# The norm's Rsqrt, its spread and the first two scaled chunks given first rank in the order of issue

## The chip, the cores and the metric

The kernel runs on one core of a Trainium2 chip. A core has engines with a queue each: TensorE (PE; its weight loads are shown apart as PEld), VectorE (DVE), ScalarE (ACT), GpSimd (POOL) and SyncE (SP), which issues most of the DMAs. The metric is device time in microseconds for one execution; less is better.

## The reference

Two layers over 256 latent tokens and 256 context tokens, 1024 wide, all in float32. `h` is the latent stream and `hc` the context stream; both go through the same weights with their own shifts and scales, and in the second layer the context stream ends after it has given its keys and values.

```python
def rms_norm(x, g):
    y = xf * lax.rsqrt(jnp.mean(xf * xf, axis=-1, keepdims=True) + EPS)
    return (y * g.astype(jnp.float32)).astype(x.dtype)
...
for l in range(DEPTH):
    h = h + 0.5 * gt1 * swiglu(modulate(rms_norm(h, g_ffn1[l]), sh1, sc1), *ffn1)
    px = modulate(rms_norm(h, g_mix[l]), sh2, sc2) @ w_in[l]
    ...   # two attentions and a long convolution on px
    h = h + gt2 * (jnp.concatenate([ya, yb, yc], axis=-1) @ w_out[l])
    h = h + 0.5 * gt3 * swiglu(modulate(rms_norm(h, g_ffn2[l]), sh3, sc3), *ffn2)
    ...   # the same for hc
```

Each feed-forward block and each mixer thus begins with an RMS norm of its input, a scale and a shift. The change touches the five norms behind the first one.

## The kernel before

**Layout.** The activations lie transposed: `self.h` holds 8 chunks (`j`) of 128 features by 512 tokens; columns 0 to 255 are stream 0 (latent), 256 to 511 stream 1 (context). Every big product is made of three matmuls in a rounded format (`mm3`, L352 to L354): high part of the weights by high part of the activations (`whi`, `xh`), high by low (`xl`), low (`wlo`) by high. `prefetch` (L323) loads weight tiles of 2048 columns (`raw`, two buffers, DMA on SP) and splits them in halves of 1024 columns: ScalarE casts `whi` (L337), VectorE subtracts for `wlo` (L338); there are four buffers of each, so that a half can be split up to four ahead of its use (`next_half`).

**The norm.** `residual` (L447, VectorE) adds a block's product to `h`; `add_square` squares the new chunk on ScalarE (L370) and adds the squares on POOL (L374). `measure` sums over the partitions with small matmuls (L385) and makes 1/rms with 11 VectorE instructions on 128 x 2 numbers (L387, L68 to L78). `spread` (L390) writes each 128 tokens' 1/rms on a diagonal (`dg`, L397, two instructions) and multiplies it with ones on TensorE (L398), so that each partition has the row `rb`. `modulate` (L428) makes, for each chunk `j`, `xn` (L439, VectorE: h by scale by `rb`), `xh` (L441, ScalarE: plus shift, rounded) and `xl` (L442, VectorE: what the rounding left).

**Order around a norm.** In the last part of a feed-forward block (`ffn`, tiles m = 2 and 3 of the down product) and of the first mixer (`mix`) stream 0 is computed ahead of stream 1, so that stream 0's norm can run beside stream 1's products: `measure(0)` and `spread(0)` stand between stream 1's products, chunks 0 to 3 of `modulate` right behind `spread(0)`, chunks 4 to 7 behind the block. Stream 1's norm hangs on hooks in the next block's first products (`pair_of_blocks`). The last mixer has stream 0 alone and does its norm in one piece at the end (`alone`). The five norms are: end of the first feed-forward block, of the first mixer, of the second and third feed-forward block, of the second mixer.

**Who orders the instructions.** The program text is a list; a planner turns it into one queue for each engine at build time. It goes through the program with its own model of times: whenever an engine is free in that model, it gets, among the instructions whose inputs and buffers are ready, the one with the lowest rank. The rank is the place in the text. Once built, an engine works its queue strictly in that order. Products go to PSUM tiles `mm` (four buffers), the norm's sums and `rb` to tiles `aux` (four buffers).

Of the kernel before, what the change touches and what calls it, by code (L numbers as in the profile page):

```python
# [41 lines left out]
class Net:  # L42
# [361 lines left out]
    def norm(self, l, which, alone=False):  # L404


        r, rb = {}, {}

        def measure(s):
            r[s] = self.measure((s,), [self.acc_tile], self.apart)  # L410

        def spread(s):
            rb[s], _ = self.spread(r[s], 2)

        def modulate(s, js):
            self.modulate(l, which, s, rb[s], js)

        if alone:
            measure(0)
            spread(0)  # L420
            modulate(0, range(ND))
            return
        self.hooks = {"measure": lambda: measure(1), "spread": lambda: spread(1), "modulate": lambda: modulate(1, range(ND))}
        return {"measure": lambda: measure(0), "spread": lambda: (spread(0), modulate(0, range(4))),
                "end": lambda: modulate(0, range(4, ND))}
# [679 lines left out]
```

## Time and profile before

| | |
|---|---|
| median of 3 runs | 1767.94 us (1767.07 to 1768.29) |
| profiled execution | 1770.06 us |
| its span, first to last instruction | 1767.4 us |
| mean granted clock of TensorE | 0.995 |
| PE busy | 1727.5 us, 98% |
| DVE busy | 1143.6 us, 65% |
| ACT busy | 649.2 us, 37% |
| POOL busy | 91.6 us, 5% |
| DMA | 251.95 MB, 143 GB/s in the mean |

The busy time counts what an engine executes; what it spends waiting for others stands beside the instruction that ended the wait. The five norms lie around 411, 663, 1031, 1407 and 1567 us of the span. A granted clock of 1.00 is 2.4 GHz, 0.50 is 1.2 GHz.

### The profile page before, as it was taken

To read this page: it belongs to the slowest core of one execution; us is meant where nothing else is said; L and a number is where in the kernel's file an instruction comes from. 1 tells how busy PE (TensorE), PEld (TensorE's weight loads), DVE (VectorE), ACT (ScalarE), POOL (GpSimd) and SP (SyncE) were. 2 spreads that over 40 slices of the span, in tenths; PEclk is the share of its full clock that TensorE was granted. 3 is DMA by queue.
4 is the path that set the end of the run, shared out by engine and by line. 5 is a ranking of instruction groups with operands and counts; after the bars stand their busy time and mean duration, and the time that the engine had idled before them with its cause. 6 is when DMAs were issued, how large, how long until landed. Compare 5 with 4: busy or idle time off the path is not lost.

```text
span 1767.4 us, 24959 instructions
## 1 busy us (share of the span) xinstructions
PE 1727.5 (98%) x9996; PEld 1479.5 (84%) x9996; DVE 1143.6 (65%) x2218; ACT 649.2 (37%) x1053; POOL 91.6 (5%) x128
## 2 busy tenths in 40 slices
PE   7999999999999999999999999999999999989999
PEld 3787888889897689888888898888888998789999
DVE  4778778757657868666676475554543587865554
ACT  4422222234337744212222342222222445744443
POOL 0000000011200020000000110000000311010000
PEclk9999999999999999999999999999999999989999
DMA  7765555532221023544544335434432233135554
GB/s 265 295 194 179 178 181 204 182 125 72 84 72 37 25 103 123 175 163 167 163 167 143 108 122 188 170 131 144 153 131 90 91 130 108 49 119 171 182 185 131
DMA packets 47430, 251.95 MB, mean 143 GB/s; under 512 B 6000, under 2 KB 7234, under 8 KB 29522
## 3 DMA queue, kind: packets, MB, share of 16 engines
q1 hardware_dynamic: 47106, 250.26, 41.0%
q8 instruction: 78, 1.28, 0.3%
q14 instruction: 38, 0.30, 0.1%
q0 software_dynamic: 64, 0.10, 0.0%
q10 hardware_dynamic: 144, 0.01, 0.0%
HBM read 249.30 MB, written 1.05 MB: 142 GB/s over the span
## 4 chain that ended last, share of the span: by engine, by line
PE 89%; DVE 7%; ACT 2%; issue 1%; DMA 1%; POOL 0%; POOLq 0%; ACTq 0%; DVEq 0%
PE mm L352 26%; PE mm L353 26%; PE mm L354 25%; DVE wlo L338 2%; PE mm L680 2%; PE mm L682 2%; PE mm L681 2%; PE aux L903 1%; PE aux L896 1%; ACT whi L337 1%; PE aux L613 1%; PE mm L872 1%; DMA raw<-wgu 0%; PE aux L125 0%; PE mm L878 0%
## 5 line engine op out<-in xcount | busy, mean ns | idle before, releaser
L352 PE MATMUL mm<-xh,whi 128*128 128x512 f32 (+1 forms) x1760 | 608.4, 350 | 9.0 <-ACT xh L441 3.8
L353 PE MATMUL mm<-xl,whi 128*128 128x512 f32 (+1 forms) x1760 | 611.0, 348 | 3.0 <-DVE xl L442 2.0
L354 PE MATMUL mm<-xh,wlo 128*128 128x512 f32 (+1 forms) x1760 | 609.9, 348 | 0.0
L338 DVE TENSOR_TENSOR wlo<-raw,whi 128x1024 fp32r<-128x1024 f32 x324 | 387.3, 1197 | 226.4 <-ACT whi L337 223.6
L337 ACT CAST whi<-raw 128x1024 fp32r<-128x1024 f32 x324 | 332.3, 1027 | 535.3 <-PE mm L353 356.8
L352 PEld LDWEIGHTS mm<-xh,whi 128*128 128x128 f32 x1760 | 332.7, 191 | 55.3 <-ACT xh L201 6.4
L353 PEld LDWEIGHTS mm<-xl,whi 128*128 128x128 f32 x1760 | 335.5, 191 | 46.8 <-DVE xl L442 2.6
L354 PEld LDWEIGHTS mm<-xh,wlo 128*128 128x128 f32 x1760 | 335.0, 191 | 42.1 <-issue 2.2
L352 PE MATMUL mm<-hh,whi 128*128 128x512 f32 (+1 forms) x788 | 271.3, 344 | 0.0
L353 PE MATMUL mm<-hl,whi 128*128 128x512 f32 (+1 forms) x788 | 271.2, 344 | 0.1
L354 PE MATMUL mm<-hh,wlo 128*128 128x512 f32 (+1 forms) x788 | 270.5, 343 | 0.0
L505 DVE TENSOR_TENSOR gs<-gs,mm 128x512 f32<-128x512 f32 (+1 forms) x88 | 54.6, 621 | 186.4 <-ACT gs L504 148.0
L352 PEld LDWEIGHTS mm<-hh,whi 128*128 128x128 f32 x788 | 149.3, 190 | 19.2 <-issue 1.9
L353 PEld LDWEIGHTS mm<-hl,whi 128*128 128x128 f32 x788 | 149.4, 190 | 18.9 <-issue 1.1
L354 PEld LDWEIGHTS mm<-hh,wlo 128*128 128x128 f32 x788 | 149.3, 189 | 17.3
L447 DVE SCALAR_TENSOR_TENSOR h<-mm,mod,h 128x256 f32<-128x256 f32 x216 | 98.7, 479 | 92.1 <-PE mm L354 91.4
L285 DVE CUSTOM_DVE_ANT_0 ada<-ada,cb 128x1024 f32<-128x1024 f32 x128 | 156.0, 1221 | 2.1
L504 ACT ACTIVATE gs<-mm 128x512 f32<-128x512 f32 (+1 forms) x88 | 47.8, 544 | 275.1 <-PE mm L354 271.2
L285 DVE CUSTOM_DVE_ANT_0 prod<-ada,cb 128x1024 f32<-128x1024 f32 x96 | 117.0, 1219 | 0.0
L374 POOL TENSOR_TENSOR acc<-acc,sq 128x256 f32<-128x256 f32 x61 | 52.5, 867 | 1237.0 <-ACT sq L370 1198.2
L680 PE MATMUL mm<-whi,xh 128*128 128x256 f32 x336 | 98.0, 292 | 0.0
L681 PE MATMUL mm<-wlo,xh 128*128 128x256 f32 x336 | 96.1, 286 | 0.0
(178 smaller groups left out, 1442.9 us busy)
## 6 DMA issues: line engine op xcount, KB each, us to landing
raw<-wgu SPq DMA_DIRECT2D x86, 1024.0 KB, 4.9
ada<-wada SPq DMA_DIRECT2D x128, 512.0 KB, 3.6
raw<-wd SPq DMA_DIRECT2D x32, 896.0 KB, 4.6
raw<-wd SPq DMA_DIRECT2D x16, 1024.0 KB, 4.9
raw<-win SPq DMA_DIRECT2D x12, 1024.0 KB, 4.8
a<-wada SPq DMA_DIRECT2D x8, 1024.0 KB, 5.0
raw<-wout SPq DMA_DIRECT2D x8, 1024.0 KB, 4.8
raw<-why SPq DMA_DIRECT2D x6, 1024.0 KB, 4.8
```

The lines of the kernel that those rows point to most:

```text
L285: nc.vector.tensor_tensor_reduce(out=prod, in0=w, in1=self.cb[:, s], scale=1.0, scalar=0.0, op0=ALU.mult, op1=ALU.add, accum_out=m[:, s, j ...
L337: nc.scalar.copy(hi[:, :n], raw)
L338: nc.vector.tensor_tensor(out=lo[:, :n], in0=raw, in1=hi[:, :n].bitcast(F32), op=ALU.subtract)
L352: t.matmul(out, whi, xhi, start=start, stop=False)
L353: t.matmul(out, whi, xlo, start=False, stop=False)
L354: t.matmul(out, wlo, xhi, start=False, stop=stop)
L374: nc.gpsimd.tensor_tensor(out=self.acc[s], in0=self.acc[s], in1=sq, op=ALU.add)
L447: return self.nc.vector.scalar_tensor_tensor(out=self.h[:, j, cols], in0=ps[:, c0:c0 + SEQ], scalar=self.mod(l, ch, s, j), in1=self.h[:, j ...
L504: nc.scalar.activation(gs[:, :n], pg[:, :n], AF.Silu)
L505: nc.vector.tensor_tensor(out=gs[:, :n], in0=gs[:, :n], in1=pu[:, :n], op=ALU.mult)
L680: nc.tensor.matmul(out, self.xh[:, kk, t], hi[:, w], start=kk == 0 and i == 0, stop=False)
L681: nc.tensor.matmul(out, self.xh[:, kk, t], lo[:, w], start=False, stop=False)
```

## The change

`high_priority()` gives all that is created inside it the rank of the start of the program, in place of its rank in the text. The change puts `measure` and `spread` of every norm in it, of both streams, and chunks 0 and 1 of stream 0's `modulate`. The first norm of all (`first_norm`) calls the inner `measure` and `spread` itself and isn't touched; nor are the squares, their sums, the residual sums, casts and splits. The instructions, their data and their buffers are the same.

```diff
         def measure(s):
-            r[s] = self.measure((s,), [self.acc_tile], self.apart)
+            with self.tc.high_priority():
+                r[s] = self.measure((s,), [self.acc_tile], self.apart)
 
         def spread(s):
-            rb[s], _ = self.spread(r[s], 2)
+            with self.tc.high_priority():
+                rb[s], _ = self.spread(r[s], 2)
 
         def modulate(s, js):
+            if s == 0 and js[0] == 0:
+                with self.tc.high_priority():
+                    self.modulate(l, which, s, rb[s], js[:2])
+                js = js[2:]
             self.modulate(l, which, s, rb[s], js)
```

## Rows read from the trace of the kernel before

**Rows 1.** The profile page, busy time of each engine in the whole span.
```profile
PE 1727.5 (98%) x9996; PEld 1479.5 (84%) x9996; DVE 1143.6 (65%) x2218; ACT 649.2 (37%) x1053; POOL 91.6 (5%) x128
```

**Rows 2.** Waits of PE: who waited for whom, total us, times, longest.
```profile
PE aux L398 <- DVE dg L397: 4.3, 3, 2.6
PE mm L352 <- ACT xh L441: 3.8, 5, 1.6
...
PE mm L353 <- DVE xl L442: 2.0, 3, 0.7
...
PE aux L385 <- POOL acc L374: 1.4, 1, 1.4
```

**Rows 3.** Windows: us; busy (count) of PE, PEld, DVE, ACT, POOL; PEclk; DMA.
```profile
395.00:425.00 30.00, 28.81 (x237) 28.20 (x236) 20.73 (x58) 11.36 (x21) 9.00 (x15) 1.00 0.22 77
650.00:680.00 30.00, 26.98 (x208) 26.25 (x207) 23.51 (x62) 12.84 (x25) 8.80 (x8) 0.94 0.20 70
...
664.00:667.00 3.00, 3.00 (x17) 3.00 (x15) 1.50 (x5) 1.16 (x3) 0.73 (x1) 0.50 0.00 0
```

**Rows 4.** Timeline of DVE, first seam: start, us, what, [idle before <- releaser].
```profile
405.09 0.28 DVE L397 TENSOR_SCALAR dg<-ident,rsy 128x128 f32<-128x128 f32 x1
405.29 2.35 DVE L338 TENSOR_TENSOR wlo<-raw,whi 128x1024 fp32r<-128x1024 f32 x2
407.56 0.87 DVE L447 SCALAR_TENSOR_TENSOR h<-mm,mod,h 128x256 f32<-128x256 f32 x2
408.35 0.28 DVE L397 TENSOR_SCALAR dg<-ident,rsy 128x128 f32<-128x128 f32 x1
409.21 0.87 DVE L439 SCALAR_TENSOR_TENSOR xn<-h,mod,aux 128x256 f32<-128x256 f32 x2 [0.58 <-PE aux L398]
410.76 1.23 DVE L338 TENSOR_TENSOR wlo<-raw,whi 128x1024 fp32r<-128x1024 f32 x1 [0.68 <-ACT whi L337]
411.91 1.00 DVE L442 SCALAR_TENSOR_TENSOR xl<-xn,mod,xh 128x256 fp32r<-128x256 f32 x2
```

**Rows 5.** Timeline of PE, first seam.
```profile
411.19 0.62 PE L352 MATMUL mm<-xh,whi 128*128 128x256 f32 x3 [0.36 <-ACT xh L441]
412.51 0.39 PE L353 MATMUL mm<-xl,whi 128*128 128x256 f32 x1 [0.70 <-DVE xl L442]
```

**Rows 6.** Timeline of PE, second seam (end of the first mixer).
```profile
658.02 0.39 PE L352 MATMUL mm<-xh,whi 128*128 128x256 f32 x1 [0.62 <-DVE h L447]
...
660.90 0.49 PE L398 MATMUL aux<-dg,ones 128*128 128x128 f32 x2 [0.82 <-DVE dg L397]
661.14 0.36 PE L352 MATMUL mm<-xh,whi 128*128 128x256 f32 x1
...
663.55 0.88 PE L352 MATMUL mm<-xh,whi 128*128 128x256 f32 x4 [1.57 <-ACT xh L441]
```

**Rows 7.** Timeline of DVE, second seam.
```profile
652.96 0.15 DVE L387 TENSOR_SCALAR ms<-aux 128x2 f32<-128x2 f32 x1
...
657.41 0.16 DVE L75 SCALAR_TENSOR_TENSOR rsy<-rsu,rsy 128x2 f32<-128x2 f32 x1
657.49 0.48 DVE L447 SCALAR_TENSOR_TENSOR h<-mm,mod,h 128x256 f32<-128x256 f32 x1
...
659.01 0.70 DVE L76 TENSOR_TENSOR rst<-rsy 128x2 f32<-128x2 f32 x1
...
661.35 1.22 DVE L338 TENSOR_TENSOR wlo<-raw,whi 128x1024 fp32r<-128x1024 f32 x1
662.48 0.86 DVE L439 SCALAR_TENSOR_TENSOR xn<-h,mod,aux 128x256 f32<-128x256 f32 x2
```

**Rows 8.** Timeline of DVE, last norm: the first and the last of 13 instructions.
```profile
1564.46 0.16 DVE L387 TENSOR_SCALAR ms<-aux 128x2 f32<-128x2 f32 x1 [0.52 <-PE aux L385]
...
1566.63 0.48 DVE L397 TENSOR_SCALAR dg<-ident,rsy 128x128 f32<-128x128 f32 x2
```

**Rows 9.** Timeline of POOL, second seam.
```profile
657.96 2.55 POOL L374 TENSOR_TENSOR acc<-acc,sq 128x256 f32<-128x256 f32 x2 [1.66 <-ACT sq L370]
```

## The prediction

> **What bounds the kernel now.** I read the page first: TensorE is busy for 98% of the span [rows 1], so the change can only win what TensorE loses around the norms. The list of waits, kept to TensorE, says what that is. Three of its lines belong to the norms: the diagonal `dg` behind `spread` (4.3 us), the scaled chunk `xh` (3.8 us) and its low part `xl` (2.0 us); no line of that list names a weight split [rows 2]. I then put stretches of 30 us around the seams (a seam: the end of one block, the norm, the start of the next) side by side: TensorE idles 30 − 28.81 = 1.19 us around the first, 3.02 us around the second, where its granted clock is 0.94 in the mean [rows 3].
>
> The order on VectorE explains the idle time at the first seam. The first half of `dg` starts at 405.09; then come two weight splits (2.35 us) and two residual sums (0.87 us), and only then the second half, at 408.35 [rows 4]. The two scaled chunks `xn` start at 409.21. Then a third split, released by ScalarE's cast, runs 1.23 us ahead of `xl` [rows 4]. TensorE loses 0.36 us until `xh` is there and 0.70 us until `xl` is [rows 5]. There are three waits for `xl`, 2.0 us in all [rows 2]: the three norms that end a feed-forward block go alike, and lose 3 × 0.36 + 2.0 = 3.1 us.
>
> The second seam (end of the first mixer) loses three pieces: 0.62 us for a residual sum, 0.82 us for `dg`, 1.57 us for `xh`, together 3.01 us [rows 6]. Here the Rsqrt chain itself is cut up: from its first instruction at 652.96 to the end of `xn` at 663.34 pass 10.4 us [rows 7]. The same chain in the last norm, with nothing between, takes from 1564.46 to 1567.11, 2.65 us [rows 8]. Behind these idle pieces the granted clock is 0.50, 1.2 GHz in place of 2.4; a mean of 0.94 over 30 us is 0.06 × 30 = 1.8 us of matmul time lost [rows 3]. This seam therefore costs 3.0 + 1.8 = 4.8 us.
>
> In the norm of the last mixer TensorE waits 2.6 us for `dg`, the longest of that line, and 1.4 us for a sum of squares on POOL [rows 2], but there the chain already runs without anything between.
>
> **The change part by part.** No instruction is added or removed, and none of the moved ones issues a DMA. What moves are, for each norm of each stream (nine in all), the measuring matmuls, 11 small VectorE instructions, two `dg` and the spreading matmuls, and for stream 0 two `xn`, `xh` and `xl`. They pass the weight splits and residual sums on VectorE, casts and squares on ScalarE, and the big matmuls in TensorE's queue; POOL's and SP's queues keep their instructions, but a weight load that waits for a delayed split goes out later by as much. I price that at nothing: the splits feed halves that lie up to four ahead, and TensorE waits for none now. Without that cover one delayed split costs its 1.2 us [rows 4].
>
> *Feed-forward seams (three).* From `dg` at 405.09 the new order on VectorE should be: both `dg` (0.48, as in [rows 8]), one split while TensorE spreads (1.2), two `xn` (0.87), the other split while ScalarE casts `xh` (1.2), two `xl` (0.9): 405.09 + 4.65 = 409.7, against 412.91 now. TensorE comes free at 411.19 − 0.36 = 410.83 [rows 5], so `xh` and `xl` of the first two chunks are there and 0.36 + 0.70 us can go. What is late next: the two residual sums (0.87) slide to 410.6 and free the accumulators late, and the third split still waits for its cast and ends near 412. TensorE bridges that with what it has, but chunks 2 and 3 follow on VectorE a split later. I leave 0.3 us per seam: 3.1 − 0.9 = 2.2 us. Bounds: nothing, if the residual sums take the whole wait over, and 3.1.
>
> *First mixer's seam.* Moving ahead does not keep the chain together: an instruction that waits for the one just before it leaves its engine free, and a ready one steps in, as the residual sum at 657.49 does behind the chain's instruction at 657.41 [rows 7]. I expect the first two splits to go on cutting in. What falls behind the chain is the third split (1.22 us, between `dg` and `xn`) and the residual sum beside it (0.48): 1.7 us earlier for `xn`, about the 1.57 us that TensorE waits for `xh`. The 0.62 and 0.82 us I leave: the first hangs on a residual sum, the second on the chain's middle. With idle time falling from 3.0 to about 1.4 us the clock may stay up: at the first seam 1.19 us of idle time leaves it at 1.00 [rows 3]. I take half of the 1.8 us. Together 1.57 + 0.9 = 2.5 us; bounds nothing and 4.8.
>
> One of the chain's instructions takes 0.70 us where its neighbour, as small, takes 0.16; a POOL sum of squares runs from 657.96 at the same time [rows 7, 9]. In the sum that stays as it is, since the POOL sums don't move. The Trainium skill (SBUF — State Buffer, section Who interferes with whom) has a VectorE instruction with two SBUF inputs wait for a whole POOL instruction that reads SBUF. By that rule a chain that runs earlier only meets other POOL sums, and the seam would give 1.57 us and no clock: 0.9 us less in all, 1764.6.
>
> *Earlier matmuls in TensorE's queue.* A measuring or spreading matmul now enters as soon as the planner thinks its input ready; where it thinks too early, everything behind it waits. At the second seam it already does so: the spreading matmul holds TensorE for 0.82 us, and the big matmuls behind it then run with no wait of their own [rows 6]. Lower bound nothing, upper bound 0.82 for each of about 12 such places, 9.8. I take 0.5 us in all, nearer to nothing, because the same order at the first seam leaves no such wait of note in the list [rows 2].
>
> *Second streams and the last norm.* TensorE waits for no second stream's norm now, so their earlier chains win nothing; they cost VectorE 2.65 us each earlier, hidden as long as chunks 2 to 7 keep ahead. The last norm's chain is clean [rows 8], and it begins when POOL's sum of squares and the squares are there, which don't move: nothing. Its 2.6 us are the chain itself.
>
> **Sum.** 2.2 + 2.5 − 0.5 = 4.2 us. The profiled execution took 1770.06 us, 2.7 more than its span; it would take 1765.9. The median of the runs is 2.1 us below the profiled one, so I forecast 1767.94 − 4.2 = 1763.7 us. A change of 0.2% (3.5 us) is about what a measurement of this kernel can tell from none.
>
> **The rivals.**
> 1. *Everything closes*: the three seams wholly (3.1), the second with its clock (4.8), less 0.5: 7.4 us, 1760.5. For it: the clock comes back whole if it never falls. Against it: splits and residual sums still step into the chain. Chance 0.13.
> 2. *The earlier chain of stream 1 takes the chunks' place.* It now runs ahead of chunks 2 to 7 of stream 0. VectorE spends about 1.8 us on two chunks (`xn` and `xl`, [rows 4]), TensorE 24 matmuls, at 28.81 us for 237 [rows 3] 2.9 us; three pairs leave 3.3 us of slack, of which a split and a residual sum take 1.7. The chain needs 2.65, so up to 1.05 us show at each of four seams: 4.2, the whole gain, and the time is 1767.9. For it: VectorE is full after 410.76 [rows 4]. Against it: the chain can begin only when the last residual sum has passed ScalarE and POOL. Chance 0.12.
> 3. *Slower: the measuring and spreading matmuls hold TensorE's queue.* At 0.82 us at each of 12 places 9.8 us are lost against 4.7 won: 1773.0. It makes the kernel slower than before from 0.39 us a place. For it: the 0.82 us [rows 6], and POOL sums that take 2.55 us for two beside a busy VectorE [rows 9], where a planner may count on less. Against it: the waits list has a measuring matmul behind POOL only once, at the last norm [rows 2]. The Trainium skill (TensorE: Matmul & The Clock Gate, section Measured speedup vs the span model) says that matmuls start and end strictly in order; the rows just named agree. Chance 0.10.
> 4. *Nothing happens*, because what is ready, not its rank, decides: 1767.9. Against it: at 405.29 a split and at 407.56 residual sums go ahead of a `dg` that was ready [rows 4]. Chance 0.08.
>
> **How the numbers follow.** The forecast has 0.57; its own range is 1761.4 to 1766.1, by one and a half or half of its two gains. Some 65% of it lies below 1764.4: 0.57 × 0.65 + 0.13 give faster 0.50; slower has most of rival 3 and a little of rival 2, 0.08; the same has the rest, 0.42. The range reaches from 1760.4, where everything closes, to 1768.2, just past rival 2 and no effect; left out are rival 3 and the outermost part of rival 1.
>
> **What would show it.** In the profile after, at the three feed-forward seams: both `dg` together, one split, two `xn`; no wait for `xh`, and little for `xl`. At the second seam: the third split behind `xn`, the wait for `xh` gone, the granted clock above 0.94. At the last norm: the same 2.6 us. Waits of the measuring matmuls for POOL's sums would speak for rival 3, waits for `xl` some 5 us behind a seam for rival 2. The forecast fails if the residual sums that slide back hold accumulators for as long as `dg` did, or if the planner's new order reaches into the attention stages.

## The result, and the profile after

The changed kernel takes 1781.94 us in the median (1780.09 to 1783.96, 5 runs) against 1767.94 us before: a ratio of 1.0081, interval 1.0070 to 1.0092. It is 14 us slower. The forecast of 1763.7 us and its range were wrong, and wrong in sign. What came is the third rival, with something added that no part of the prediction had.

From `modulate` on the changed kernel's line numbers are 6 higher: `xn` is L445, `xh` L447, `xl` L448, the residual sum L453. The page's busy times are these:

```profile
PE 1734.5 (97%) x9996; PEld 1485.4 (83%) x9996; DVE 1143.5 (64%) x2218; ACT 648.1 (36%) x1053; POOL 94.5 (5%) x128
```

The span grew from 1767.4 to 1781.9 us, by 14.5. TensorE is busy 7.0 us longer for the same 9996 matmuls [rows 1], and idle for 47.4 us in place of 39.9, 7.5 more: the loss is half waiting and half a lower clock. The waits of TensorE, in the columns of [rows 2]:

```profile
PE aux L385 <- POOL acc L374: 10.5, 9, 2.6
PE aux L398 <- DVE dg L397: 5.0, 5, 2.6
...
PE aux L385 <- ACT sq L370: 1.3, 1, 1.3
PE mm L352 <- ACT xh L447: 1.1, 1, 1.1
```

Four of the five waits for `xh` are gone, and all for `xl`. In their place the measuring matmul L385 waits nine times for a sum of squares on GpSimd, 10.5 us in all; before it did so once, for 1.4 us. The spreading matmul's waits for `dg` grew too, from 4.3 to 5.0 us. (0.9 us of the new idle time is not the change's: a wait for `xh` in the first norm, which it leaves alone, took 4.3 us in place of 3.4.) TensorE's timeline shows where the sums are waited for (the rows at 620.47 and 1479.15 are landmarks between the seams, used below):

```profile
401.86 0.61 PE L385 MATMUL aux<-inv_d,acc 128*128 128x2 f32 x4 [0.52 <-POOL acc L374]
...
418.59 0.78 PE L385 MATMUL aux<-inv_d,acc 128*128 128x2 f32 x4 [2.63 <-POOL acc L374]
...
620.47 0.51 PE L352 MATMUL mm<-xh,whi 128*128 128x512 f32 x1 [0.70 <-ACT pr L897]
...
656.85 0.61 PE L385 MATMUL aux<-inv_d,acc 128*128 128x2 f32 x4 [0.52 <-POOL acc L374]
...
1040.08 1.01 PE L385 MATMUL aux<-inv_d,acc 128*128 128x2 f32 x4 [1.51 <-POOL acc L374]
...
1422.04 0.71 PE L385 MATMUL aux<-inv_d,acc 128*128 128x2 f32 x4 [2.65 <-POOL acc L374]
...
1479.15 0.63 PE L751 MATMUL aux<-ident,qraw 128*128 128x128 f32 x4 [1.45 <-DVE qraw L740]
...
1573.99 0.38 PE L385 MATMUL aux<-inv_d,acc 128*128 128x2 f32 x2 [1.38 <-POOL acc L374]
1576.77 1.01 PE L385 MATMUL aux<-inv_d,sq 128*128 128x2 f32 x4 [1.34 <-ACT sq L370]
```

At a feed-forward seam the first such wait is stream 0's (0.52 us), the last is stream 1's (2.63, 1.51 and 2.65 us). The windows, in the columns of [rows 3], show what follows the long ones:

```profile
395.00:425.00 30.00, 26.34 (x201) 25.54 (x201) 18.58 (x53) 10.20 (x19) 9.71 (x15) 0.94 0.24 83
650.00:680.00 30.00, 28.62 (x226) 27.18 (x225) 22.83 (x59) 12.54 (x25) 10.65 (x12) 1.00 0.21 71
418.80:422.20 3.40, 3.40 (x18) 3.40 (x18) 2.76 (x12) 0.97 (x2) 0.00 (x0) 0.51 0.66 275
1040.10:1046.90 6.80, 6.80 (x32) 6.80 (x33) 4.16 (x19) 0.97 (x2) 0.00 (x0) 0.50 0.66 235
1422.30:1425.70 3.40, 3.40 (x18) 3.40 (x18) 2.91 (x10) 0.97 (x2) 0.00 (x0) 0.51 0.62 263
1575.90:1589.50 13.60, 8.97 (x39) 8.62 (x40) 8.78 (x27) 3.50 (x8) 0.00 (x0) 0.50 0.23 77
```

The two seams have changed places. The second one, in the mixer, now has a clock of 1.00 and 1.38 us of idle time in 30 (before 0.94 and 3.02 [rows 3]); the first has 0.94 and 3.66 us (before 1.00 and 1.19). Behind stream 1's three long waits the granted clock is 0.50, 1.2 GHz, for 3.4, 6.8 and 3.4 us, and behind the last norm's waits for 13.6. Before, the second seam had 3.4 us of it [rows 3] and the last norm 10.2:

```profile
1565.10:1575.30 10.20, 7.12 (x31) 6.85 (x32) 6.96 (x22) 2.38 (x5) 0.00 (x0) 0.50 0.24 96
```

Between the first two seams each trace has one more stretch of 3.4 us, before around 583 us and after around 485, and the two cancel.

To price each seam by itself, compare the times of the same instructions in both traces. On VectorE, the product behind `gs` ahead of the first seam, ahead of the third, ahead of the fourth, and behind the last norm; before:

```profile
370.48 0.69 DVE L505 TENSOR_TENSOR gs<-gs,mm 128x512 f32<-128x512 f32 x1 [2.70 <-ACT gs L504]
...
990.13 0.69 DVE L505 TENSOR_TENSOR gs<-gs,mm 128x512 f32<-128x512 f32 x1 [3.38 <-ACT gs L504]
...
1366.10 0.69 DVE L505 TENSOR_TENSOR gs<-gs,mm 128x512 f32<-128x512 f32 x1 [3.38 <-ACT gs L504]
...
1583.92 0.75 DVE L505 TENSOR_TENSOR gs<-gs,mm 128x256 f32<-128x256 f32 x2 [0.28 <-ACT gs L504]
```

and after:

```profile
370.90 0.69 DVE L511 TENSOR_TENSOR gs<-gs,mm 128x512 f32<-128x512 f32 x1 [2.69 <-ACT gs L510]
...
993.16 0.69 DVE L511 TENSOR_TENSOR gs<-gs,mm 128x512 f32<-128x512 f32 x1 [3.38 <-ACT gs L510]
...
1374.36 0.69 DVE L511 TENSOR_TENSOR gs<-gs,mm 128x512 f32<-128x512 f32 x1 [3.38 <-ACT gs L510]
...
1598.40 0.75 DVE L511 TENSOR_TENSOR gs<-gs,mm 128x256 f32<-128x256 f32 x2 [0.28 <-ACT gs L510]
```

and two of TensorE's in the mixers before, which answer to 620.47 and 1479.15 above:

```profile
615.12 0.51 PE L352 MATMUL mm<-xh,whi 128*128 128x512 f32 x1 [0.70 <-ACT pr L891]
...
1466.92 0.63 PE L745 MATMUL aux<-ident,qraw 128*128 128x128 f32 x4 [1.44 <-DVE qraw L734]
```

The changed kernel is 0.42 us late ahead of the first seam, then 5.35, 3.03, 8.26, 12.23 and 14.48. So the first seam (with the mixer behind it) costs 4.9 us, the second **gives 2.3**, the third costs 5.2, the fourth 4.0 and the last norm 2.2. These are two executions, one of each kernel; how far they can be trusted is taken up with the prediction below.

Why is the sum of squares late? GpSimd's timeline at the first seam, before:

```profile
408.69 1.56 POOL L374 TENSOR_TENSOR acc<-acc,sq 128x256 f32<-128x256 f32 x2 [4.84 <-ACT sq L370]
410.92 3.77 POOL L664 TENSOR_TENSOR tabs<-rope,gqk 128x64 f32<-128x64 f32 x8 [0.67 <-PE mm L354]
414.74 0.82 POOL L374 TENSOR_TENSOR acc<-acc,sq 128x256 f32<-128x256 f32 x1
```

and after:

```profile
411.54 0.75 POOL L374 TENSOR_TENSOR acc<-acc,sq 128x256 f32<-128x256 f32 x1 [5.96 <-ACT sq L370]
412.50 2.49 POOL L670 TENSOR_TENSOR tabs<-rope,gqk 128x64 f32<-128x64 f32 x4 [0.21 <-PE mm L354]
414.95 0.73 POOL L374 TENSOR_TENSOR acc<-acc,sq 128x256 f32<-128x256 f32 x1
415.64 2.21 POOL L670 TENSOR_TENSOR tabs<-rope,gqk 128x64 f32<-128x64 f32 x4
417.81 0.72 POOL L374 TENSOR_TENSOR acc<-acc,sq 128x256 f32<-128x256 f32 x1
```

`tabs` are eight small products of the rotary table and its gains, which the mixer behind the seam needs; they hang on nothing in the seam. Before, all eight ran while GpSimd had no square to add, and the last sum ended at 415.56. After, the squares come later, the eight are cut in two groups that stand between the sums, and the last sum ends at 418.53, 2.97 us later (0.42 us of it was there ahead of the seam). The last square itself starts only 0.84 us later, at 415.02 in place of 414.18: the rest is the second group of `tabs`, 2.21 us, which stands ahead of its sum. VectorE shows why the squares are late:

```profile
404.95 0.91 DVE L397 TENSOR_SCALAR dg<-ident,rsy 128x128 f32<-128x128 f32 x2
406.47 0.87 DVE L445 SCALAR_TENSOR_TENSOR xn<-h,mod,aux 128x256 f32<-128x256 f32 x2 [0.61 <-PE aux L398]
...
408.39 0.96 DVE L448 SCALAR_TENSOR_TENSOR xl<-xn,mod,xh 128x256 fp32r<-128x256 f32 x2
...
410.41 0.87 DVE L453 SCALAR_TENSOR_TENSOR h<-mm,mod,h 128x256 f32<-128x256 f32 x2
```

This is the order that was forecast, with `xl` ready at 409.35 (forecast 409.7). But the two residual sums that stood at 407.56 [rows 4] now start at 410.41, and from each of them hangs a square on ScalarE, a sum on GpSimd, and stream 1's measuring matmul.

### The profile page after: what moved, and what is told of

It reads as the page before. It is cut to its first block, busy times and chain, and to the rows that moved or that the text cites. A ratio compares the mean times of both kernels' runs of the same rounds, so it can differ in the third digit from the quotient of the medians.

```text
span 1781.9 us, 24959 instructions
## 1 busy us (share of the span) xinstructions
PE 1734.5 (97%) x9996; PEld 1485.4 (83%) x9996; DVE 1143.5 (64%) x2218; ACT 648.1 (36%) x1053; POOL 94.5 (5%) x128
## 4 chain that ended last, share of the span: by engine, by line
PE 89%; DVE 6%; ACT 2%; POOL 1%; issue 1%; POOLq 0%; DMA 0%; ACTq 0%; DVEq 0%
PE mm L352 25%; PE mm L353 25%; PE mm L354 25%; PE mm L686 2%; PE mm L687 2%; PE mm L688 2%; PE aux L909 1%; PE aux L902 1%; DVE wlo L338 1%; PE aux L619 1%; ACT whi L337 1%; POOL acc L374 1%; PE aux L385 1%; PE mm L878 1%; PE aux L398 0%
## 5 line engine op out<-in xcount | busy, mean ns | idle before, releaser
L352 PEld LDWEIGHTS mm<-xh,whi 128*128 128x128 f32 x1760 | 336.3, 192 | 52.8 <-ACT xh L201 6.4
L453 DVE SCALAR_TENSOR_TENSOR h<-mm,mod,h 128x256 f32<-128x256 f32 x216 | 98.8, 479 | 84.3 <-PE mm L354 83.4
```

The source lines that it names most:

```text
L352: t.matmul(out, whi, xhi, start=start, stop=False)
L453: return self.nc.vector.scalar_tensor_tensor(out=self.h[:, j, cols], in0=ps[:, c0:c0 + SEQ], scalar=self.mod(l, ch, s, j), in1=self.h[:, j ...
```

## The experiments

Two theories, both needed or either enough. **Theory 1:** the measuring matmuls enter TensorE's queue too early and hold it for GpSimd's sum. **Theory 2:** the sum itself comes later, since the residual sums stand behind the chunks, and `tabs` steps in between. A third was that stream 1's Rsqrt goes ahead of stream 0's chunks. All ratios are to the kernel before, run on the same chip; "waits" are the measuring matmuls' for GpSimd's sums, in all (before: 1.4 us, once). "At text rank" means at its place in the program text, as before the change.

| kernel | median us | ratio, interval | waits, us (times) |
|---|---|---|---|
| changed | 1781.94 | 1.0081 (1.0070 to 1.0092) | 10.5 (9) |
| e1 measure at text rank | 1777.35 | 1.0053 (1.0038 to 1.0067) | 5.9 (4) |
| e2 only the measuring matmuls ahead | 1772.85 | 1.0031 (1.0019 to 1.0042) | 7.0 (9) |
| e3 as changed, matmuls at text rank | 1775.81 | 1.0039 (1.0024 to 1.0054) | 5.7 (4) |
| e4 stream 0 alone | 1775.65 | 1.0043 (1.0028 to 1.0058) | 7.9 (8) |
| e5 only the chunks ahead | 1766.81 | 0.9999 (0.9989 to 1.0008) | 0.4 (1) |
| e6 only the spread ahead | 1769.87 | 1.0013 (1.0003 to 1.0022) | 2.0 (2) |
| x1 changed, tables behind | 1779.14 | 1.0066 (1.0052 to 1.0080) | 8.2 (9) |
| h1 changed, residual sums ahead | 1778.48 | 1.0055 (1.0040 to 1.0070) | 8.8 (9) |
| h2 both of these | 1771.84 | 1.0026 (1.0016 to 1.0035) | 5.4 (9) |
| n1 changed, last norm at text rank | 1777.75 | 1.0051 (1.0034 to 1.0067) | 9.5 (9) |
| x2 measure at text rank, tables behind | 1769.11 | 1.0009 (0.9999 to 1.0018) | 2.1 (3) |
| c0 before, tables behind | 1767.51 | 0.9994 (0.9985 to 1.0003) | 0.4 (1) |
| b2 stream 0 alone, measure ahead only in the mixer | 1772.51 | 1.0027 (1.0017 to 1.0037) | 6.4 (5) |
| b1 b2 with tables behind | 1764.88 | 0.9990 (0.9981 to 0.9999) | 1.6 (4) |

**e1: measure back at its place in the text** (against the changed kernel).

```diff
-            with self.tc.high_priority():
-                r[s] = self.measure((s,), [self.acc_tile], self.apart)
+            r[s] = self.measure((s,), [self.acc_tile], self.apart)
```

> The whole of measure (its matmuls and the Rsqrt) goes back to its rank in the text; spread and the first two chunks stay at first rank. Theory 1 (the measuring matmuls enter TensorE's queue too early and hold it for POOL's sum): the 10.5 us of waits for POOL fall to the 1.4 us of the last norm, the gains at the seams stay, 1761 to 1765 us. Theory 2 (POOL's sums themselves come late, because residual sums and squares are pushed behind the chunks): the measuring matmuls of stream 1 go on waiting 1 us or more at each feed-forward seam, 1772 us or more.

A third of the loss went, no more. Stream 0's 0.52 us waits and the third seam's 1.51 us went, but at the first and fourth seam stream 1's matmul still waits, 1.82 and 3.45 us. There GpSimd shows the table products between the sums; the fourth seam of this kernel:

```profile
1411.55 0.74 POOL L374 TENSOR_TENSOR acc<-acc,sq 128x256 f32<-128x256 f32 x1
1412.24 1.77 POOL L669 TENSOR_TENSOR tabs<-rope,gqk 128x64 f32<-128x64 f32 x2
1413.97 0.90 POOL L374 TENSOR_TENSOR acc<-acc,sq 128x256 f32<-128x256 f32 x1
1414.84 0.59 POOL L669 TENSOR_TENSOR tabs<-rope,gqk 128x64 f32<-128x64 f32 x2
1415.39 0.72 POOL L374 TENSOR_TENSOR acc<-acc,sq 128x256 f32<-128x256 f32 x1
```

So a measuring matmul at its old place can be too early as well, if the sum has moved.

**e2: the kernel before, with the measuring matmuls alone ahead.**

```diff
+                with self.tc.high_priority() if first else nullcontext():
-                nc.tensor.matmul(pt[:, 2 * i:2 * i + 2], part, self.inv_d, ...)
+                    nc.tensor.matmul(pt[:, 2 * i:2 * i + 2], part, self.inv_d, ...)
```

> The kernel before, with the measuring matmuls alone at first rank; Rsqrt, spread and chunks at their rank in the text. Theory 1: about 0.5 us of wait at each stream 0 and 0.5 to 2.6 us at each stream 1, and a clock that falls behind the longer ones, with none of the gain: 1775 to 1785 us. Theory 2: nothing pushes the sums back, so no wait worth naming and 1766 to 1770 us.

The matmuls alone cost 0.31%, 5.5 us: the nine waits are there (0.52 us for stream 0 at each seam; 0.40, 1.17, 1.51 and 0.42 for stream 1; 1.38 at the last norm), and 1.34 us for ScalarE's square behind them. Theory 1 has a part of its own, without any chunk ahead, though the time lies between the two forecasts (1775 to 1785 and 1766 to 1770 us). The gain comes as well: at the three feed-forward seams no wait for `xh` or `xl` is left, and at the mixer's 0.23 and 1.10 us of them, with the clock at 1.00.

**e3: Rsqrt ahead, its measuring matmuls not** (against the changed kernel; the rest of `measure`, behind the matmuls, stands in `high_priority`, and the matmuls do not).

> As the changed kernel, but the measuring matmuls alone at their rank in the text; the Rsqrt stays at first rank. Theory 1: as the run with the whole measure in the text, 1761 to 1765 us. Theory 2: 1772 us or more. Theory 3 (the Rsqrt of stream 1 goes ahead of stream 0's chunks on VectorE and TensorE waits for xl): slower than the run with the whole measure in the text by 2 us or more, with waits for xh or xl some 5 us behind a seam.

The interval overlaps with that of e1, and the waits are e1's within 0.2 us (1.83 and 3.27 us at the first and fourth seam). Whether Rsqrt is ahead makes no difference that shows: the third theory is dropped.

**e4: first rank for stream 0 alone.**

```diff
-            with self.tc.high_priority():
+            with self.tc.high_priority() if s == 0 else nullcontext():
```

(in `measure` and in `spread`)

> First rank for stream 0's norms alone (the last norm too); stream 1's measure and spread at their rank in the text. Theory 1: the waits of stream 1 (2.63 + 0.21 + 1.51 + 2.65 = 7.0 us) and the half clock behind them (13.7 us of it, 6.8 us lost) go, the 0.52 us at each stream 0 stay: about 1768 us. Theory 2: stream 1's sums are still pushed back by stream 0's chunks: 1774 us or more.

Stream 1's matmul now stands at its text rank, and still waits 1.21 and 3.01 us at the first and fourth seam. What makes it wait is stream 0's chain ahead of the residual sums: theory 2.

**e5 and e6: one part alone**, the chunks or the spread.

> One part alone: only the first two scaled chunks of a norm are queued ahead; measuring matmul, Rsqrt and spread stay at their place in the program text. If the chunks alone push the residual sums back far enough to make GpSimd's sums late, stream 1's measuring matmul waits over 1 us at two seams and the time is 1771 us or more. If it needs the spread ahead as well, no such wait shows and the time is 1765 to 1768 us.

> One part alone: only the spread of 1/rms is queued ahead (its two diagonal products and two matmuls, both streams); measuring matmul, Rsqrt and chunks at their place in the program text. Chunks alone changed nothing, so this tells which of the two carries the gain and the loss. If the pair of parts is needed for either, 1766 to 1769 us with the waits for xh and xl at the seams about as before; if the spread carries the loss, 1771 us or more with stream 1's measuring matmul waiting over 1 us; if it carries the gain without the loss, 1765 us or less.

The chunks alone change nothing: the waits of [rows 5, 6] are there to 0.01 us. A chunk can't go before the spread that it reads, and behind it it is already next. The spread alone takes away the waits for `xh` and `xl` at all three feed-forward seams (0.23 us for `dg` is left) and brings a wait of 1.61 us for the sum at the fourth. At the mixer's seam it wins nothing: the waits there are 0.62, 0.82, 0.76 and 0.83 us. This is none of the three cases as they were written: it carries the gain and a share of the loss, and they cancel.

**x1, x2 and c0: the table products behind the seam's last sum**, in the changed kernel, in e1 and in the kernel before.

```diff
+                        with self.tc.issue_after(getattr(self.last_add, "ins", self.last_add)):
-                        nc.gpsimd.tensor_tensor(out=tabs[:, q, tt, w], in0=self.rope[:, tt, w], ...)
+                            nc.gpsimd.tensor_tensor(out=tabs[:, q, tt, w], in0=self.rope[:, tt, w], ...)
```

> The changed kernel, with the eight table products of GpSimd at a seam put behind that seam's last sum of squares; nothing else is different. Theory 2 (GpSimd's sums come late because the residual sums stand behind the chunks, and the table products then step in between the sums): stream 1's measuring matmul waits 1.5 us or less at the first and the fourth seam, as at the third, where there are no tables, in place of 2.63 and 2.65; the half clock behind 418 and 1422 us goes, and the time is 1776 to 1780 us. If the tables are innocent, the two waits stay over 2.3 us and the time is within 2 us of the changed kernel's 1781.9.

> Measuring matmuls at their place in the program text, spreads and the first chunks ahead, and the table products behind the last sum of squares. If both causes are as thought (the matmuls enter TensorE's queue too early; the tables step in between GpSimd's sums), stream 1's waits of 1.8 and 3.4 us at the first and the fourth seam fall to 0.5 us or less, the half clock behind 417 and 1417 us goes, and the time is 1769 us or less. If the tables are innocent, the waits stay and the time is 1774 us or more.

> A control: the kernel before, with only the table products put behind the seam's last sum of squares. If they harm only where the residual sums are late, there is nothing to win here (no wait of TensorE for GpSimd's sum at these seams before) and the time is within 1.5 us of the kernel before. If the tables cost time of their own, it is 2 us or more faster.

In x1 stream 1's waits fell as expected, to 1.52 and 1.47 us, the size of the third seam's; but half clock still follows at both seams, and the time fell by less than 3 us. In x2 nearly all of the loss is gone: 1.0009, the first seam's wait is away and the fourth's is 1.47 us, where 0.5 was expected. The control c0 is not to be told from the kernel before: the tables cost nothing where the squares come on time. Between e1 and x2 they cost 7.8 us (1.0053 less 1.0009, of 1768).

**h1 and h2: stream 1's residual sums and squares ahead too**, alone and with the tables behind (against the changed kernel).

```diff
-                            self.residual(pt, l, 5, j, s, i * SEQ)
-                            self.add_square(j, s)
+                            with self.tc.high_priority() if s == 1 else nullcontext():
+                                self.residual(pt, l, 5, j, s, i * SEQ)
+                                self.add_square(j, s)
```

(the same in `ffn`)

> The changed kernel, with stream 1's residual sums and squares of the last step before each norm queued ahead too, so that they stand one or two places earlier among the scaled chunks on VectorE; the table products stay between GpSimd's sums. If the residual sums behind the chunks are what makes the last sum late, stream 1's waits of 2.63 and 2.65 us at the first and fourth seam fall to 1.6 us or less, and the time is 1775 to 1779 us. If only the table products count, the waits stay over 2.3 us and the time is 1780 us or more.

> The changed kernel with both: stream 1's residual sums and squares ahead, and the table products behind the last sum of squares. Measuring matmuls stay ahead. If late sums are all that makes stream 1's measuring matmul wait, its waits fall to 0.5 us or less at all four seams (2.10, 0.76, 0.24 and 2.26 us with the first of the two alone), and what is left is the 0.5 us of stream 0 at each seam and the last norm: 1771 to 1775 us. If the matmuls' early place is enough for them, waits of 1 us or more stay at two seams and the time is 1776 us or more.

With h1 the third seam's 1.51 us falls to 0.24, while the first and fourth keep 2.10 and 2.26, where 1.6 or less was expected: there the tables still stand between. With both, the early matmul hardly waits at the feed-forward seams. GpSimd at the first seam of h2:

```profile
412.47 1.39 POOL L374 TENSOR_TENSOR acc<-acc,sq 128x256 f32<-128x256 f32 x1 [1.36 <-ACT sq L370]
414.52 0.73 POOL L374 TENSOR_TENSOR acc<-acc,sq 128x256 f32<-128x256 f32 x1 [0.67 <-ACT sq L370]
415.22 3.70 POOL L672 TENSOR_TENSOR tabs<-rope,gqk 128x64 f32<-128x64 f32 x8
```

and its measuring matmul:

```profile
415.31 0.61 PE L385 MATMUL aux<-inv_d,acc 128*128 128x2 f32 x4 [0.17 <-POOL acc L374]
```

The waits of stream 1 are 0.17, 0.77, 0.24 and 0.25 us; 0.5 or less was expected, and the mixer's seam alone is above. No half clock follows at any seam, and the time is in the range expected. From 1.0081 to 1.0026 is 9.7 us: that is what late sums cost.

**n1: the last norm's `measure` at its text rank**, the seams as changed.

```diff
-            with self.tc.high_priority():
+            with nullcontext() if alone else self.tc.high_priority():
```

> The changed kernel with the last norm's measuring matmul and Rsqrt back at their place in the program text; the four seams are unchanged. If the early matmuls cost time there by themselves, the waits of 1.38 and 1.34 us become 0.4 and 0.5 us as in the runs that left them at their place, the half clock behind them is 10.2 us long in place of 13.65, and the time is 1777 to 1780 us. If the waits there are only the same work waited for elsewhere, the time is within 1.5 us of the changed kernel's 1781.9.

The waits are 0.43 and 0.53 us, the half clock behind them 10.2 us long, and the median is 4.2 us below the changed kernel's (by the ratios 5.3). In the two traces the last norm itself accounts for 3.0 us of this: from the landmark at 1479.15 to the product behind the norm the changed kernel takes 119.25 us, n1 116.23. At the last norm there is no second stream, and spread and chunks stay ahead in n1: what is left is `measure`'s early place, and in e2 the matmuls' place alone brings the same two waits. h2 still has them (1.88 and 1.34 us); that its remaining 4.6 us are theirs is not shown, since no run has both edits.

**b1 and b2: what won, without what lost.** The spread and the first chunks are ahead for stream 0 alone, the measuring matmul for stream 0 at the mixer's seam alone; b1 has the tables behind, b2 not.

```diff
         def measure(s):
-            with self.tc.high_priority():
+            with self.tc.high_priority() if s == 0 and which == 2 and not alone else nullcontext():
...
         def spread(s):
-            with self.tc.high_priority():
+            with self.tc.high_priority() if s == 0 else nullcontext():
```

> The parts that won, without those that lost: spread and first chunks ahead for stream 0 alone, the measuring matmul ahead for stream 0 at the mixer's seam alone, stream 1 wholly at its place in the program text, table products behind the last sum of squares. If the two causes are all there is, the waits for xh and xl at the mixer's seam go (3.0 us of idle TensorE and its half clock of 3.4 us), no wait for GpSimd's sum over 0.6 us takes their place, and the time is 1763 to 1766 us. If there is a third cause, 1770 us or more.

> The best version so far without its move of the table products: spread and first chunks ahead for stream 0, measuring matmul ahead for stream 0 at the mixer's seam alone. If the tables between the sums are needed for the loss, stream 1's waits for GpSimd's sum at the first and fourth seam come back at 1.5 us or more each with half clock behind them, and the time is 1769 to 1775 us; if not, it stays at 1763 to 1766 us.

b1 takes 1764.88 us, 0.9990 of the kernel before (0.9981 to 0.9999): the best here, within what was expected, and barely told from no change. Its windows around the first two seams, in the columns of [rows 3]:

```profile
395.00:425.00 30.00, 29.39 (x241) 28.71 (x239) 22.74 (x60) 11.80 (x22) 9.58 (x15) 1.00 0.21 71
650.00:680.00 30.00, 28.82 (x227) 27.64 (x228) 26.42 (x68) 14.27 (x28) 7.23 (x8) 1.00 0.20 70
```

Idle time is 0.61 and 1.18 us, against 1.19 and 3.02 before, with the clock at 1.00 in both. Without the tables' move, in b2, the waits of 1.83 and 3.46 us are back, and it is 1.0027: the same kernel but for the place of two groups of eight small products, on an engine that is busy for 5% of the span, is 6.5 us slower.

## Why the prediction was wrong, point by point

**What bounds the kernel, and the feed-forward order: right.** The waits of [rows 5] were there to be won, and the order on VectorE came out as forecast. The 2.2 us can't be read as such, since the same seams lost far more. In e6, where the gain stands almost by itself, TensorE idles 0.29 and 0.23 us in 30 at the first and third seam, in place of 1.19 and 1.11: 0.9 us a seam, where 0.7 was forecast; the stretches between the landmarks get shorter by 0.3 and 0.6 us. That the chunks' own rank had a part in it was wrong: e5 gives nothing, and the spread alone (e6) or the measuring matmuls alone (e2) take the waits away.

**First mixer's seam: nearly right in size, wrong in mechanism.** 2.5 us were forecast and 2.3 measured, but that is luck. The split between `dg` and `xn` was to fall behind the chain, and the first two were to go on cutting in. It came the other way round: the chain on VectorE, from 10.4 us [rows 7], takes 5.6, the first two splits are out of it, and one still stands between `dg` and `xn`:

```profile
657.50 0.16 DVE L387 TENSOR_SCALAR ms<-aux 128x2 f32<-128x2 f32 x1 [1.36 <-PE aux L385]
...
660.22 0.95 DVE L397 TENSOR_SCALAR dg<-ident,rsy 128x128 f32<-128x128 f32 x2
661.09 1.21 DVE L338 TENSOR_TENSOR wlo<-raw,whi 128x1024 fp32r<-128x1024 f32 x1
662.23 0.86 DVE L445 SCALAR_TENSOR_TENSOR xn<-h,mod,aux 128x256 f32<-128x256 f32 x2
```

(The 2.65 us that the prediction set against the 10.4 ends with `dg` and not with `xn`; to the end of `xn` the last norm's chain took 4.7.) Nor does first rank on VectorE do it: in e3 Rsqrt, spread and chunks have it, the chain takes 9.4 us, and TensorE waits 0.69, 0.87, 0.52 and 1.00 us. The stretch between the landmarks at 615.12 and 990.13 takes 375.01 us before, 372.69 in the changed kernel, but 376.09, 376.14 and 375.74 in e1, e3 and e6, where the measuring matmul is not ahead, and 373.95 in e2, where it alone is. So the early matmul, the term that was booked as a cost, brings the gain here. The waits of 0.62 and 0.82 us, which were left as they were, went with it, and 0.52 us for the measuring matmul came. The clock stayed up wholly in place of half, but that need not be the change's: in e5 the waits are those of [rows 6], no half clock follows, and the stretch takes 373.65 us, 1.36 less than before. Idle time was forecast at 1.4 us, and is 1.38, made up otherwise.

The 0.70 us instruction of [rows 7] is gone: none of the small ones takes over 0.17. GpSimd ran nothing between 656.80 and 660.35. That agrees with the rule cited from the Trainium skill (SBUF — State Buffer, section Who interferes with whom); what was wrong is the conclusion drawn from it, that an earlier chain meets other sums.

**The step that failed: "Earlier matmuls in TensorE's queue".** It was taken as 0.5 us. The new waits are 10.4 us (10.5 for GpSimd and 1.3 for ScalarE, less the 1.4 of [rows 2]), and 0.7 more for `dg`, before the clock is counted. The reason given, that "the same order at the first seam leaves no such wait of note in the list [rows 2]", was no evidence: the order in that trace was that of the text, where a measuring matmul stands behind the products between which the text puts it, and that distance is what kept it from waiting. Stream 1's at the first seam started at 417.29, 1.73 us after the sum it reads had ended at 415.56. With the first rank only the planner's own times hold it back, and it comes too early: by 0.52 us for stream 0 at each seam, where nothing else had moved. This slack was the figure to weigh. Rival 3, which had the mechanism, named [rows 9] (two sums in 2.55 us, where one by itself can take 0.73) and was given 0.10.

**"Since the POOL sums don't move": wrong.** The residual sums were seen to slide, and were priced at 0.3 us a seam for the accumulators they hold. Their real price is the chain behind them, square, sum and measuring matmul; at the first seam its last sum ends 2.97 us later. By h1, x1 and h2 the lateness has two parts, each enough to keep a wait: taking away one saves 2.7 to 4.6 us, taking away both 9.7. That `tabs` was there to step in could be read from the trace before, and was not looked at.

**"Second streams and the last norm: nothing": wrong.** Stream 1's measuring matmuls have the longest waits. The last norm lost 2.2 us in the two traces, 3.0 against n1's. Against c0's it is 3.9: the stretch that takes 117.00 us in the trace before takes 115.32 there, with nothing changed at that norm, so one execution differs from another by 1.7 us.

**Rival 3 was the right one and too small**, 1773.0. Nine waits came where 12 were counted, and at 1.17 us (10.5 / 9) they are longer than its 0.82; above all it left the clock out. Half clock behind three seams and the longer stretch at the last norm (3.4 + 6.8 + 3.4, and 13.6 in place of 10.2) less the 3.4 us that the second seam no longer has is 13.6 us; a stretch at half clock in which TensorE is busy throughout costs half its length, so that this is 6.8 us at the most, and TensorE was busy 7.0 longer. (The rule on the order of matmuls that this rival cites stands on the page named, TensorE: Matmul & The Clock Gate of the Trainium skill, in the section The mechanism.)

**Left open:** how much of b1's gain is the change's. Its interval reaches from 0.2 to 3.4 us, and the control c0, with none of the change in it, is at 0.9994 with an interval that overlaps. Of the 2.35 us by which b1's stretch from the landmark at 615.12 to that at 990.13 is shorter, e5 has 1.36 without any shorter wait.

## What to carry to other kernels

An instruction that gets first rank in a queue worked in order must be late only for itself: before a matmul is put ahead, look at the slack that its input has in the trace, not at whether it waits now, since its present place may be what hides the input's lateness. When work is pushed back to make room, follow its chain to the end over all engines and price the last link, not only the buffers it holds. And look at what the planner may put into the gap on the nearly idle engine: here two groups of eight products on an engine at 5% decided over 6.5 us.

## What the runs showed of the hardware that was not expected

The same wait at the same place had different prices by the clock. In the changed kernel 1.51 us of waiting at the third seam is followed by 6.8 us at a granted clock of 0.50 (window 1040.10 to 1046.90). In x1 the wait there is 1.52 us and none follows, while the first seam, also with 1.52 us, has 6.8 us of it; windows of x1 behind the first seam's wait and around the third's:

```profile
416.80:423.60 6.80, 6.80 (x32) 6.80 (x33) 4.59 (x19) 0.97 (x2) 2.45 (x8) 0.50 0.46 157
1036.00:1043.00 7.00, 5.48 (x46) 5.28 (x45) 5.50 (x22) 2.18 (x5) 1.56 (x1) 1.00 0.87 335
```

At half their length these stretches are worth 3.4 us, at one seam or at another, in two kernels that wait alike: more than the 1.06 us of waiting [rows 5] that was to be won at such a seam. The third seam bears this out: from the landmark at 990.13 to the one at 1366.10 it costs 5.2 us in the changed kernel and 2.2 in x1. Nor does a longer wait always bring half clock: in e4 3.01 us of waiting at the fourth seam is followed by none (clock 1.00 from 1411 to 1428 us), and in e5 none follows the 3.0 us at the mixer's seam. What decides it isn't shown here.
